# Six weight tiles that began at the same place in a 256-byte line, moved to six different places

## The chip, the core and the metric

The kernel runs on one core of a Trainium2 chip. Its time is the device time of one execution in microseconds (us): lower is better. Each execution does the whole layer, from inputs in device memory to the output in device memory.

The core has a matrix engine (PE, with its weight loads shown apart as PEld), a vector engine (DVE), an activation engine (ACT), a general engine (POOL), a queue that issues transfers (SP), and 16 DMA engines. The four engines work out of one on-chip memory of 128 partitions. "Offset" below always means the byte within a partition at which a tile begins.

## What is computed

One layer of an encoder on 512 frames of 1024 channels, in float32. Cut to its products:

```python
proj = x @ w_in                                    # queries, keys, values, gates of two mixers
y_a = sparse attention (indexer, top 128 keys, relative bias, softmax)   # 8 heads of 64
y_s = stick-breaking attention (strictly causal)                        # 8 heads of 64
merged = sigmoid(g_a + b_a) * (y_a @ w_branch_dsa) + sigmoid(g_b + b_b) * (y_s @ w_branch_sb)
x = layer_norm(alpha * x + merged @ w_out)
u, g = split(x @ w_ffn_in)                         # 2 x 2816 channels
h = gelu(causal_conv3(u)) * g
x = layer_norm(alpha * x + h @ w_ffn_out)
```

## The kernel before, in words

**Products in three passes.** PE takes its operands in a rounded 32-bit format. To keep the accuracy of float32, every operand is split in two: a high part (the value copied into the rounded format) and a low part (the value minus the high part). A product is then three matmuls into one accumulator: high by high, high by low and low by high. So each weight that comes from memory is loaded, split by two elementwise instructions, and used by three matmuls for each slice of 128.

**The stream of weights.** All weights pass through one object, `Stream`, in one fixed order of pieces of up to 128 x 1024 values. `load` (line 75) fetches pieces ahead into the pool `rawp` (three buffers of 128 x 1024 float32), through the SP queue at line 73. `_advance` (line 88) splits them, up to three ahead of their use: line 104 writes the high part on ACT; the low part is written by DVE (line 113), by POOL for the five pieces in `POOL_LO` (the same line), or, for the 14 pieces in `DMA_LO`, by ACT with minus the high part (line 107) and then a DMA that adds the weight itself into the tile (line 110).

**The ring.** The split parts stand in the pool `ring`: three buffers with the tag `whi` and three with the tag `wlo`, allotted at lines 98 and 99. These six buffers are all that the change touches. A few pieces have places of their own instead (`self.place`): the eight of the output projection and eleven of the last 24. Everything else uses the ring.

**Who reads the ring.** As the stationary operand (the weights that PE loads): the projections at lines 312 to 314 (384 columns) and 233 to 235 (512 columns), the branch projections at lines 611 to 613 and 817 to 819, and the feed-forward input `ffn_in` at lines 937 to 939. As the moving operand (what streams through PE): the value projections at lines 270 to 272 and the feed-forward output, `product`, at lines 1017 to 1019.

**Stages in time.** Up to about 322 us, projections, indexer and both attentions are interleaved: the attention of a head keeps DVE, ACT, POOL and the transposing DMAs (`send_planes`, line 478; `join_planes`, line 487) busy, and projections from the list `FILL` keep PE busy meanwhile. Then come the last gates and the branch products (to about 345 us), the output projection `o_ps` (lines 866 to 868), the first norm, the feed-forward pairs `u`/`g` with the first output products (about 391 to 674 us), the remaining output products (to about 732 us) and the last norm.

**The order on each engine** is set when the program is built, by a list scheduler with a model of times, with ties written by hand (`issue_after`).

**Where tiles lie.** Pools are stacked from the left side in the order in which they are opened: constants, `rawp`, `ring`, and behind them the pools of each stage (`bp` for the attentions, `cp`, `tp`, then `ep`, `fp`, `hp`, `rp`). Others are stacked from the right side (`xp`, `dp`, `qp`, `wp`). A helper, `padded`, rounds small tiles up to 128 bytes. In the built program each `raw` tile and each of the six ring tiles begins 192 bytes into a line of 256 bytes, since each is 4096 bytes long.

Of the kernel before, what the change touches and what calls it, by code (L numbers as in the profile page):

```python
# [12 lines left out]
F32R = mybir.dt.float32r  # L13
# [35 lines left out]
def r32(ap):  # L49
    return ap.bitcast(F32)  # L50


class Stream:
# [34 lines left out]
    def _advance(self, upto):  # L88
        nc = self.nc
        n = len(self.pieces)  # L90
        self.load(min(n, upto + self.al))
        while self.ns < min(n, upto + self.asp, self.nl):
            t, w = self.loaded.pop(self.ns)
            key = self.pieces[self.ns][0]
            if key in self.place:
                hi, lo = self.place[key](key)
            else:
                hi = self.ring.tile([128, 1024], F32R, tag="whi", name=f"whi_{self.ns}")
                lo = self.ring.tile([128, 1024], F32R, tag="wlo", name=f"wlo_{self.ns}")
            after = None  # L100
            if key in self.prepare:
                w, after = self.prepare[key](t)
            with self.tc.issue_after(self.behind) if self.behind is not None else nullcontext():
                self.high = nc.scalar.activation(hi[:, :w], t[:, :w], AF.Copy).ins  # L104
            self.behind = None
            if key in self.lo_by_dma:
                self.high = self.highs[key] = nc.scalar.activation(lo[:, :w], r32(hi[:, :w]), AF.Copy, scale=-1.0).ins
                if key == "gb6":
                    self.behind = self.high
                self.done[key] = nc.gpsimd.dma_start(lo[:, :w], self.pieces[self.ns][1], accum_op=ALU.add).ins  # L110
            else:
                eng = nc.gpsimd if key in self.lo_on_pool else nc.vector
                self.done[key] = eng.tensor_sub(lo[:, :w], t[:, :w], r32(hi[:, :w])).ins  # L113
            if after is not None:
                after()
            self.split[self.ns] = (hi, lo)
            self.ns += 1
# [1181 lines left out]
```

## Times and profile before

| | |
|---|---|
| two timed runs | 746.85 and 747.27 us, median 747.06 us |
| span of the profiled execution, first to last instruction | 744.9 us |
| PE busy | 735.6 us, 99% |
| DVE busy | 572.0 us, 77% |
| ACT busy | 408.0 us, 55% |
| POOL busy | 148.8 us, 20% |
| mean granted PE clock | 0.998 |

The profiled execution's own time is its span, 744.9 us; the median of the timed runs is 2.2 us longer, which is what lies before the first and after the last profiled instruction. In the rows of the profile, a line number is that of the kernel, `whi<-raw` means that a tile named `whi` is written from one named `raw` (buffer numbers are left out), `x` a count, and the last field of a row the idle time just before the instruction with what ended it. Matmuls overlap, so the duration of one (389 ns) is longer than the step from one start to the next.

### The profile page before, as it was taken

How to read it: one execution, taken by the hardware profiler on the slowest of the kernel's cores; microseconds unless marked ns; L12 is line 12 of the kernel's file. 1: busy time of each engine (PE TensorE's matmuls, PEld its weight loads, DVE VectorE, ACT ScalarE, POOL GpSimd, SP SyncE). 2: the span in 40 equal slices, each digit the busy share in tenths (PEclk: the TensorE clock that was granted, in tenths of full speed). 3: DMA queues.
4: the chain of work that ended last, by engine and by line, in shares of the span. 5: the costliest groups of instructions: out<-in, count | busy, mean ns of one | idle time of the engine just before them, and what ended most of it. 6: DMA issues, size and time to landing. Idle time of an engine off the chain costs nothing.

```text
span 744.9 us, 9755 instructions
## 1 busy us (share of the span) xinstructions
PE 735.6 (99%) x3477; PEld 616.9 (83%) x3477; DVE 572.0 (77%) x907; ACT 408.0 (55%) x572; POOL 148.8 (20%) x161
## 2 busy tenths in 40 slices
PE   9999999999999999999999999999999999999995
PEld 7888888888888888888889888888888888888885
DVE  5569888999679898668755866686767668668985
ACT  6466867797785587845473533443444344345430
POOL 0002224365743332000101111011101101110011
PEclk9999999999999999999999999999999999999999
DMA  7445887796476455527832544444443444448632
GB/s 266 157 128 188 207 172 173 158 214 163 116 181 154 135 126 136 131 85 247 289 57 86 170 141 142 141 143 143 141 166 114 161 136 149 144 140 268 202 130 84
DMA packets 73631, 117.03 MB, mean 157 GB/s; under 512 B 42536, under 2 KB 42792, under 8 KB 73584
## 3 DMA queue, kind: packets, MB, share of 16 engines
q1 hardware_dynamic: 66304, 93.98, 42.0%
q0 software_dynamic: 5744, 18.38, 9.9%
q10 hardware_dynamic: 1536, 4.06, 2.1%
q8 instruction: 27, 0.44, 0.3%
q14 instruction: 20, 0.16, 0.1%
HBM read 95.93 MB, written 9.98 MB: 142 GB/s over the span
## 4 chain that ended last, share of the span: by engine, by line
PE 89%; DVE 3%; POOL 2%; issue 2%; DMA 2%; ACT 2%; DVEq 0%; POOLq 0%; ACTq 0%
PE u_ps L937 5%; PE u_ps L939 5%; PE g_ps L937 5%; PE u_ps L938 5%; PE g_ps L939 5%; PE g_ps L938 5%; PE m L1019 2%; PE m L1017 2%; PE m L1018 2%; PE av_ps L511 2%; PE ga_ps L234 2%; PE ga_ps L233 2%; PE gb_ps L235 2%; PE gb_ps L234 2%; PE ga_ps L235 2%; PE gb_ps L233 2%
## 5 line engine op out<-in xcount | busy, mean ns | idle before, releaser
L104 ACT ACTIVATE whi<-raw 128x1024 fp32r<-128x1024 f32 (+1 forms) x124 | 123.8, 1001 | 143.1 <-PE g_ps L938 43.7
L113 DVE TENSOR_TENSOR wlo<-raw,whi 128x1024 fp32r<-128x1024 f32 (+1 forms) x105 | 123.9, 1181 | 36.3 <-ACT whi L104 35.6
L939 PE MATMUL u_ps<-x1h,wlo 128*128 128x512 f32 (+1 forms) x192 | 71.4, 372 | 0.0
L937 PE MATMUL u_ps<-x1h,whi 128*128 128x512 f32 (+1 forms) x192 | 71.3, 372 | 0.0
L938 PE MATMUL u_ps<-x1l,whi 128*128 128x512 f32 (+1 forms) x192 | 71.3, 371 | 0.0
L937 PE MATMUL g_ps<-x1h,whi 128*128 128x512 f32 (+1 forms) x184 | 69.9, 380 | 0.0
L938 PE MATMUL g_ps<-x1l,whi 128*128 128x512 f32 (+1 forms) x184 | 69.9, 380 | 0.0
L939 PE MATMUL g_ps<-x1h,wlo 128*128 128x512 f32 (+1 forms) x184 | 69.9, 380 | 0.0
L939 PEld LDWEIGHTS u_ps<-x1h,wlo 128*128 128x128 f32 x192 | 36.2, 188 | 6.3
L938 PEld LDWEIGHTS u_ps<-x1l,whi 128*128 128x128 f32 x192 | 36.2, 188 | 6.3
L937 PEld LDWEIGHTS u_ps<-x1h,whi 128*128 128x128 f32 x192 | 36.2, 188 | 6.2
L939 PEld LDWEIGHTS g_ps<-x1h,wlo 128*128 128x128 f32 x184 | 34.6, 188 | 6.6
L938 PEld LDWEIGHTS g_ps<-x1l,whi 128*128 128x128 f32 x184 | 34.6, 188 | 6.5
L937 PEld LDWEIGHTS g_ps<-x1h,whi 128*128 128x128 f32 x184 | 34.6, 188 | 6.5
L960 DVE TENSOR_TENSOR t<-raw 128x512 f32<-128x512 f32 x11 | 7.6, 693 | 40.1 <-DMA raw<-in_w_fo_dram 39.2
L569 POOL TENSOR_TENSOR bm<-win,score 128x256 f32<-128x256 f32 (+2 forms) x24 | 26.9, 1147 | 32.2 <-DMA pl<-bm 27.3
L985 ACT ACTIVATE c<-c,cwt 128x512 f32<-128x512 f32 x22 | 15.9, 725 | 27.5 <-DVE c L984 27.3
L979 POOL MEMSET u<- 128x2 f32 x22 | 2.1, 98 | 143.7 <-ACT whi L104 99.2
L993 DVE TENSOR_TENSOR hF<-g_ps,c 128x512 f32<-128x512 f32 x22 | 15.1, 687 | 19.7 <-PE g_ps L939 19.7
L835 POOL TENSOR_TENSOR rstd<-rstd,mhalf 128x1 f32<-128x1 f32 x8 | 7.7, 959 | 104.6 <-DVE rstd L834 104.6
L423 DVE MAX8 m<-score 128x8 f32<-128x256 f32 (+2 forms) x48 | 26.6, 556 | 0.9
L557 POOL TENSOR_TENSOR beta<-beta,keep 128x1280 f32<-128x1280 f32 x8 | 21.6, 2704 | 26.7 <-DVE keep L554 26.7
(576 smaller groups left out, 2088.3 us busy)
## 6 DMA issues: line engine op xcount, KB each, us to landing
raw<-in_w_fi_dram SPq DMA_DIRECT2D x44, 512.0 KB, 3.3
raw<-in_w_t_dram SPq DMA_DIRECT2D x32, 512.0 KB, 3.7
raw<-in_w_fo_dram SPq DMA_DIRECT2D x26, 512.0 KB, 4.2
wlo<-in_w_t_dram POOLq DMA_DIRECT2D x14, 512.0 KB, 5.8
raw<-in_w_br_dram SPq DMA_DIRECT2D x8, 512.0 KB, 4.0
raw<-in_w_o_dram SPq DMA_DIRECT2D x8, 512.0 KB, 4.1
raw<-in_w_v_dram SPq DMA_DIRECT2D x7, 512.0 KB, 4.6
raw_b<-in_w_fo_dram SPq DMA_DIRECT2D x6, 512.0 KB, 5.5
```

The costliest lines, as they stand in the source:

```text
L104: self.high = nc.scalar.activation(hi[:, :w], t[:, :w], AF.Copy).ins
L113: self.done[key] = eng.tensor_sub(lo[:, :w], t[:, :w], r32(hi[:, :w])).ins
L233: nc.tensor.matmul(ps[:M], wh[:, c], xh[k], start=(k == 0), stop=False)
L234: nc.tensor.matmul(ps[:M], wh[:, c], xl[k], start=False, stop=False)
L235: nc.tensor.matmul(ps[:M], wl[:, c], xh[k], start=False, stop=(k == KC - 1))
L423: nc.vector.max(m8, sc)
L557: nc.gpsimd.tensor_mul(beta, beta, keep[:, 1:ATT + 1])
L569: nc.gpsimd.tensor_add(bm[:, OFF[j]:OFF[j] + N], win[:, 512 - N:512], score[j])
L937: nc.tensor.matmul(ps[:, c], wh[:, kc], x1h[:, k, c], start=(k == 0), stop=False)
L938: nc.tensor.matmul(ps[:, c], wh[:, kc], x1l[:, k, c], start=False, stop=False)
L939: nc.tensor.matmul(ps[:, c], wl[:, kc], x1h[:, k, c], start=False, stop=(k == KC - 1))
L985: nc.scalar.activation(c, c, AF.Gelu_apprx_tanh, bias=cwt[:, f, 3:4])
```

## The change

```diff
@@ -95,8 +95,8 @@
             if key in self.place:
                 hi, lo = self.place[key](key)
             else:
-                hi = self.ring.tile([128, 1024], F32R, tag="whi", name=f"whi_{self.ns}")
-                lo = self.ring.tile([128, 1024], F32R, tag="wlo", name=f"wlo_{self.ns}")
+                hi = self.ring.tile([128, 1032], F32R, tag="whi", name=f"whi_{self.ns}")
+                lo = self.ring.tile([128, 1032], F32R, tag="wlo", name=f"wlo_{self.ns}")
             after = None
             if key in self.prepare:
                 w, after = self.prepare[key](t)
```

Each ring tile becomes 4128 bytes long. What is written and read of it stays the first 1024 values. In the two built programs the instructions of PE, DVE, ACT, POOL and SP, and their order, are the same row for row; only offsets differ:

| tiles | offset within 256 bytes before | after |
|---|---|---|
| `raw` (pool `rawp`) and all constants | 192 (`raw`) | unchanged |
| `whi`, the three buffers in the order in which they lie | 192, 192, 192 | 192, 224, 0 |
| `wlo`, the three buffers in the order in which they lie | 192, 192, 192 | 32, 64, 96 |
| tiles behind the ring that were at 192 (for example `beta`, `win`, `mh`, `bh`, `wo`) | 192 | 128 |
| tiles behind the ring that were at 64 (for example `xr`, `raw_qi`, `q`, `k`, `keep`/`bm`, `pl`, `back`) | 64 | 0 |
| tiles stacked from the right side (`xh`, `xl`, `x1h`, `x1l`, the norm's tiles) | 64 or 192 | unchanged |

Before the change every tile that PE reads begins at a multiple of 64 bytes. After it, one `whi` buffer (224) and two `wlo` buffers (32 and 96) begin 32 bytes off such a multiple.

## The prediction

> **What bounds the kernel now.** First the page's head.
>
> ```profile
> span 744.9 us, 9755 instructions
> PE 735.6 (99%) x3477; PEld 616.9 (83%) x3477; DVE 572.0 (77%) x907; ACT 408.0 (55%) x572; POOL 148.8 (20%) x161
> ```
>
> PE is busy nearly throughout. A busy PE may still run below its best rate, so the second view is the list of PE's waits (total, count, longest).
>
> ```profile
> PE idle_ps L210 <- DVE idle L207: 1.2, 1, 1.2
> PE bs_ps L613 <- DVE wlo L113: 0.3, 1, 0.3
> PE qi_ps L312 <- ACT whi L104: 0.3, 1, 0.3
> ```
>
> Only two waits lie on the ring, 0.3 us each. So the time can change in two ways only: the step from one matmul to the next changes, or some splitting engine becomes late enough that PE waits where it now doesn't. For the step, starts from the timeline of PE: the 24 matmuls of one feed-forward input, 12 of the output projection, and, from the chain of waits, three of 384 columns.
>
> ```profile
> 501.44 0.39 PE L937 MATMUL g_ps<-x1h,whi 128*128 128x512 f32 x1
> 506.88 0.39 PE L937 MATMUL u_ps<-x1h,whi 128*128 128x512 f32 x1
> ```
>
> ```profile
> 380.15 0.39 PE L867 MATMUL o_ps<-wo0l,mh 128*128 128x512 f32 x1
> 382.87 0.39 PE L867 MATMUL o_ps<-wo4l,mh 128*128 128x512 f32 x1
> ```
>
> ```profile
> 11.22 0.52 PE qi_ps L314 x3
> ```
>
> With the ring as weights: 5.44 / 24 = 0.2267 us. Without any ring tile (`wo` and `mh` have places of their own): 2.72 / 12 = 0.2267 us. With 384 columns: 0.52 / 3 = 0.173 us. The 128 columns between are worth 0.053 us, 0.417 ns each, so 512 columns take 213.5 ns and some 13 ns of each step do not depend on the columns.
>
> The step is thus the same to a tenth of a nanosecond whether or not PE reads the ring. In the first stretch the ring is also written: the instructions on `whi` alone, in that window, are these (busy us and count on PE, PEld, DVE, ACT, POOL).
>
> ```profile
> 501.40:506.90 5.50, 4.99 (x18) 3.02 (x18) 1.23 (x1) 1.06 (x1) 0.00 (x0) 1.00 0.72 245
> ```
>
> One split on ACT and one on DVE went on beside 18 matmuls from the same ring. If the common offset made the six tiles collide with each other, the first stretch would be the longer. That is the main evidence that there is nothing here for a new offset to win.
>
> **The change part by part.** Nothing is removed or added, and the order on every engine is the same, so no wait is new and no transfer is issued at another place. What remains is the price of an instruction at another offset, for each reader and writer of the moved tiles.
>
> *Weights on PE.* How long a weight load really takes shows where a matmul is too short to cover it, in five short matmuls of one attention head:
>
> ```profile
> 97.81 0.28 PE L511 MATMUL av_ps<-pth,vs 128*128 128x256 f32 x1
> 97.92 0.28 PE L511 MATMUL av_ps<-ptl,vs 128*128 128x256 f32 x1
> 98.05 0.23 PE L511 MATMUL av_ps<-pth,vs 128*128 128x128 f32 x1
> 98.11 0.27 PE L511 MATMUL av_ps<-ptl,vs 128*128 128x128 f32 x1
> 98.22 1.25 PE L540 MATMUL z_ps<-ks1a,qs1a 128*128 128x512 f32 x7
> ```
>
> 128 columns should take 53 + 13 = 67 ns, and one step is 60 ns, but the next is 110: the load is behind, and takes about 0.11 us. Under a step of 0.2267 it has 0.117 us to spare; even a load twice as long would be hidden there. My estimate for the weights is 0; if loads from shifted tiles were half as long again (0.165), the 384-column steps (0.173) would still cover them.
>
> *Moving operands on PE.* 512 values are 2048 bytes of a row in either case. The trace has no operand of PE off a multiple of 64 bytes. Of the two sorts it has (192, as in the stretches above, and 64, as `vs`, `qs` and `pth` here), neither is slower: two 256-column steps from 97.81 to 98.05 are 0.12 us each, and 256 x 0.417 + 13 = 120 ns. I take 0; the upper bound is the first rival.
>
> *Splits on ACT, DVE and POOL.* These engines do have rows at odd offsets: the convolution reads `u` 4 and 8 bytes past a tile's start (L983, L984), beside the norm's like instruction (L839); ACT writes `u` at 8 bytes (L980), beside a copy to a tile's start (L1155); POOL multiplies by `keep` from 4 bytes on (L557), beside an addition from tiles' starts (L569).
>
> ```profile
> L839 DVE SCALAR_TENSOR_TENSOR r<-r,mv,ln x14: 741/746/751, 363.7 to 734.8; 128x512 f32<-128x512 f32 x14
> ```
>
> ```profile
> L983 DVE SCALAR_TENSOR_TENSOR c<-u,cwt,c x22: 743/750/1401, 406.8 to 670.1; 128x512 f32<-128x512 f32 x22
> ```
>
> ```profile
> L984 DVE SCALAR_TENSOR_TENSOR c<-u,cwt,c x22: 739/752/753, 408.6 to 671.9; 128x512 f32<-128x512 f32 x22
> ```
>
> ```profile
> L980 ACT ACTIVATE u<-u_ps 128x512 f32<-128x512 f32 x22 | 12.8, 581 | 0.0
> L1155 ACT ACTIVATE m<-P 128x512 f32<-128x512 f32 x2 | 1.1, 583 | 0.0
> ```
>
> ```profile
> L557 POOL TENSOR_TENSOR beta<-beta,keep 128x1280 f32<-128x1280 f32 x8 | 21.6, 2704 | 26.7 <-DVE keep L554 26.7
> L569 POOL TENSOR_TENSOR bm<-win,score 128x512 f32<-128x512 f32 x8 | 11.0, 1380 | 0.0
> ```
>
> Medians (the middle of three numbers) of 750 and 752 against 746 ns on DVE; 581 against 583 on ACT; on POOL 2704 / 1280 = 2.1 ns a value against 1380 / 512 = 2.7. So between a gain of nothing and a loss of 6 ns per 512 values on DVE, and no loss on ACT and POOL. I take 0, since a step of 32 bytes is coarser than these. Where it would be paid is the one stretch in which the chain of waits leaves PE (start, length, what):
>
> ```profile
> 189.56 0.19 PE ka_ps L233
> ...
> 191.01 3.63 POOL wlo L113
> ...
> 195.64 0.17 POOL wlo L113
> ...
> 209.95 0.96 ACT whi L104
> ...
> 210.93 1.68 DVE wlo L113
> ...
> 224.85 2.23 DVE wlo L113
> ...
> 228.51 1.22 DVE wlo L113
> ...
> 231.88 5.88 DMA pl<-bm
> ...
> 245.59 3.55 DMA pl<-bm
> ...
> 254.31 1.55 PE l_ps L580 x8
> ```
>
> The splits in it sum to 3.63 + 0.17 + 0.96 + 1.68 + 2.23 + 1.22 = 9.89 us, and the scores `l_ps` at 254.31 wait for its end, so a split longer by some share costs PE that share of 9.89 us. The four splits on DVE and ACT at 6 ns per 512 values, 12 each, cost under 0.05 us. Elsewhere there is cover: in a steady stretch of the feed-forward DVE is busy 70.77 of 100 us and its splits are 26.85 of that (the second row is `wlo` alone), so they could double and still end in time, at 97.6.
>
> ```profile
> 420.00:520.00 100.00, 100.00 (x443) 82.81 (x442) 70.77 (x93) 40.50 (x51) 13.75 (x20) 1.00 0.44 148
> ```
>
> ```profile
> 420.00:520.00 100.00, 57.19 (x148) 27.44 (x147) 26.85 (x24) 0.00 (x0) 0.00 (x0) 1.00 0.44 148
> ```
>
> *Transfers.* Fourteen low parts are finished by a DMA into the ring; and tiles behind the ring move too, among them both ends of the transposes `pl<-bm`:
>
> ```profile
> wlo<-in_w_t_dram POOLq DMA_DIRECT2D x14, 512.0 KB, 5.8
> pl<-bm SPq DMA_TRANSPOSE x16, 3.5
> ```
>
> A 4096-byte row from byte 192 touches 17 lines of 256 bytes; from 32, 64 or 96 it touches 17 as well. So the fourteen should keep their 5.8 us. The transposes go from 64 to 0; no row shows one from a line's start, so I bound them by nothing and by all that PE could win, below.
>
> The Trainium skill, "DMA: Bandwidth & Descriptors", section "How a descriptor splits into AXI transactions", has a rule for this: a descriptor is cut at 256-byte addresses, and one that starts off such an address pays for the bytes before its start. By it a piece of 256 bytes at 64 takes two transactions and at 0 one, so the transposes would shorten. No row here shows it either way; the result would be the second rival's.
>
> *Sum.* Weights 0, moving operands 0, splits 0, transfers 0: the span stays 744.9 us, and with the 2.2 us around it (median 747.06 less 744.9) the time stays **747.1 us**. Without a change in the step, what could add up is small on both sides: minus 0.5 us (the waits before `bs_ps` and `l_ps`) to plus 1 us (a tenth more on the chain's splits), 746.6 to 748.1.
>
> **The rivals.** *1. A row that begins 32 bytes off a multiple of 64 costs PE a second start: slower.* The counts of matmuls on `whi` and on `wlo`:
>
> ```profile
> 0.00:745.00 745.00, 550.61 (x1826) 337.10 (x1826) 134.90 (x118) 148.46 (x151) 14.06 (x5) 1.00 0.54 157
> ```
>
> ```profile
> 0.00:745.00 745.00, 346.79 (x913) 171.17 (x913) 134.90 (x118) 14.73 (x14) 26.32 (x19) 1.00 0.54 157
> ```
>
> One of three `whi` buffers and two of three `wlo` buffers are so placed: 1826 / 3 + 913 x 2 / 3 = 1217 matmuls. At a second 13 ns each that is 15.8 us, all of it on PE: 762.9 us. From 12.3 ns a matmul on (15 / 1217) the kernel is slower by over 2%. For it: nothing in the trace has tried such an offset on PE. Against it: offsets 64 and 192 give the same step, and the other engines read 4 bytes past a start as fast.
>
> *2. The tiles behind the ring gain: slightly faster.* If the two transposes on the chain (5.88 and 3.55 us) took half, the chain would shorten by 4.7 us, but PE wins only what it waits: 0.3 us before L613, and 0.23 before `l_ps`, whose step from the matmul ahead is 254.31 - 253.85 = 0.46 instead of 0.23.
>
> ```profile
> 253.85 0.39 PE L613 MATMUL bs_ps<-ys3h,wlo 128*128 128x512 f32 x1
> ```
>
> That gives 746.5 us.
>
> *3. The splits lengthen the chain: slower within 2%.* A quarter on each of the splits between 191 and 231 us costs 9.89 / 4 = 2.5 us: 749.6 us. For it: this stretch has no slack. Against it: the rows at odd offsets.
>
> *4. The 13 ns are a collision that the change ends: faster.* If the new offsets took them off each of the 1826 + 913 = 2739 matmuls that read the ring, that would be 35.6 us: 711.5 us. For it: the 13 ns are there on every step. Against it: `o_ps` has the same 13 ns without the ring, and 256 columns from the ring-free `pth` too.
>
> The Trainium skill, "TensorE: Matmul & The Clock Gate", section "Back-to-back issue gap", gives N / 2.4 + 2.5 ns, which is 215.8 for 512 columns. By it 10.9 of the 226.7 would be too much, and rival 4 would come to 717.2 us; this trace has 226.7 with and without the ring, so the page's lower figure does not point at the ring.
>
> **How the numbers follow.** Unchanged 0.78, rival 2 0.07, rival 3 0.07, rival 1 0.07 (0.04 of it at over 2%), rival 4 0.01. The prediction is the likeliest, 747.1 us. The range takes in its bounds, rivals 2 and 3 and a small part of rival 1 (3 ns a matmul, 3.7 us, 750.8): 745.5 to 750.8. Below 746.5 it allows 1 us for runs that differ (the two runs are 0.4 apart). Faster by over 2% 0.01, slower by over 2% 0.04, within 2% (about what a measurement of this kernel can tell from no change) 0.95.
>
> **What would show it.** Right: steps of 0.2267 us in 937 to 939 and in 1017 to 1019, medians of L104 and L113 within 1%, the same two short waits of PE. Rival 1 shows as longer steps on a third of the weights' matmuls and two thirds of `wlo`'s, at best in 1017 to 1019. Rival 2 shows as shorter landings of `pl<-bm`, rival 3 as longer L113 or L104 and a larger PE wait near 227 and 254 us. The prediction is wrong if any row at a moved offset differs from its like before by more than a few per cent, or if the span moves by over 4 us.

## The result and the profile after

The changed kernel takes 757.79 us (median of two runs, 757.65 and 757.93) against 747.06: a ratio of 1.0139, with a 95% interval of 1.0120 to 1.0158. It is slower by 1.4%, 10.7 us, and lies outside the predicted range of 745.5 to 750.8. The profiled execution's span went from 744.9 to 755.9 us at the same mean granted clock, 0.998.

The head of the page after, and the whole list of PE's waits:

```profile
span 755.9 us, 9755 instructions
PE 746.9 (99%) x3477; PEld 617.2 (82%) x3477; DVE 570.6 (75%) x907; ACT 408.8 (54%) x572; POOL 148.8 (20%) x161
```

```profile
PE idle_ps L210 <- DVE idle L207: 1.2, 1, 1.2
```

PE is busy 11.3 us longer with the same 3477 matmuls, and both short waits on the ring are gone, as a slower PE gives the splits more time. So nothing is late. The matmuls themselves take longer, and it shows in their groups with shapes kept apart (busy us, mean ns of one); each of these three means was 389 before.

```profile
L937 PE MATMUL g_ps<-x1h,whi 128*128 128x512 f32 x168 | 66.6, 397 | 0.0
L939 PE MATMUL g_ps<-x1h,wlo 128*128 128x512 f32 x168 | 66.1, 394 | 0.0
L938 PE MATMUL g_ps<-x1l,whi 128*128 128x512 f32 x168 | 65.8, 392 | 0.0
```

The weight loads, as the profile records them, did not become longer: each takes 188 ns on average, and only the idle time between loads grew. These are the loads of the high parts for the inputs `g`, before and then after:

```profile
L937 PEld LDWEIGHTS g_ps<-x1h,whi 128*128 128x128 f32 x184 | 34.6, 188 | 6.5
```

```profile
L937 PEld LDWEIGHTS g_ps<-x1h,whi 128*128 128x128 f32 x184 | 34.6, 188 | 7.1
```

Matmuls overlap, so the step from start to start is the price. In the timeline of PE after, these are the first matmuls of four feed-forward inputs, 24 matmuls apart:

```profile
427.60 0.39 PE L937 MATMUL g_ps<-x1h,whi 128*128 128x512 f32 x1
...
433.19 0.40 PE L937 MATMUL u_ps<-x1h,whi 128*128 128x512 f32 x1
...
438.78 0.40 PE L937 MATMUL g_ps<-x1h,whi 128*128 128x512 f32 x1
...
444.33 0.39 PE L937 MATMUL u_ps<-x1h,whi 128*128 128x512 f32 x1
```

The distances are 5.59, 5.59 and 5.55 us, where before 24 matmuls took 5.44. The output projection, whose operands `mh` and `wo` moved together from 192 to 128, did not change at all; 12 of its matmuls:

```profile
383.70 0.39 PE L867 MATMUL o_ps<-wo0l,mh 128*128 128x512 f32 x1
...
386.42 0.39 PE L867 MATMUL o_ps<-wo4l,mh 128*128 128x512 f32 x1
```

That is 2.72 us as before. The steps of all matmuls, summed by the lines of the kernel in both traces (the last column is the difference divided by the count, 256-column and shorter matmuls included):

```
lines                              before    after    difference    a matmul
937-939    feed-forward input      240.49   245.89   +5.40 us      4.8 ns x 1128
233-235    projections             181.46   184.69   +3.23         4.1 ns x 792
1017-1019  feed-forward output     105.09   106.95   +1.86         3.8 ns x 494
270-272    value projections        44.21    44.76   +0.55
312-314    qi, ki                   16.86    17.04   +0.19
611-613, 817-819  branches          44.79    44.71   -0.08
866-868    output projection        43.52    43.55   +0.03
the rest (attention and others)     59.49    59.11   -0.37
sum                                735.91   746.70   +10.8
```

The loss is here, on the lines that read the ring with 512 columns. The branches read it with 512 columns too, and they paid like the others: their median step went from 227 to 232 ns. Their sum stood still only because pauses in their stretch went at the same time: what single steps over 245 ns have above 227 fell from 1.0 to 0.2 us, PE's former wait at L613 among it. The other moved work stood still; the splits and transfers after:

```profile
L104 ACT ACTIVATE whi<-raw 128x1024 fp32r<-128x1024 f32 (+1 forms) x124 | 123.9, 1003 | 162.9 <-PE g_ps L938 48.8
L113 DVE TENSOR_TENSOR wlo<-raw,whi 128x1024 fp32r<-128x1024 f32 (+1 forms) x105 | 124.1, 1184 | 42.4 <-ACT whi L104 41.0
```

```profile
wlo<-in_w_t_dram POOLq DMA_DIRECT2D x14, 512.0 KB, 5.5
pl<-bm SPq DMA_TRANSPOSE x16, 3.3
```

The splits' means were 1001 and 1181 ns, the landings 5.8 and 3.5 us.

### The profile page after: what moved, and what is told of

Its sections match the earlier page's. It is cut to its first block, busy times and chain, and to the rows that moved or that the text cites. A ratio compares the mean times of both kernels' runs of the same rounds, so it can differ in the third digit from the quotient of the medians.

```text
span 755.9 us, 9755 instructions
## 1 busy us (share of the span) xinstructions
PE 746.9 (99%) x3477; PEld 617.2 (82%) x3477; DVE 570.6 (75%) x907; ACT 408.8 (54%) x572; POOL 148.8 (20%) x161
## 4 chain that ended last, share of the span: by engine, by line
PE 93%; DVE 3%; DMA 1%; ACT 1%; issue 1%; ACTq 0%; DVEq 0%
PE g_ps L937 5%; PE u_ps L939 5%; PE u_ps L937 5%; PE u_ps L938 5%; PE g_ps L939 5%; PE g_ps L938 5%; PE m L1017 2%; PE m L1018 2%; PE m L1019 2%; PE av_ps L511 2%; PE ga_ps L233 2%; PE ga_ps L234 2%; PE ga_ps L235 2%; PE o_ps L866 2%; PE o_ps L867 2%; PE o_ps L868 2%
## 5 line engine op out<-in xcount | busy, mean ns | idle before, releaser
L104 ACT ACTIVATE whi<-raw 128x1024 fp32r<-128x1024 f32 (+1 forms) x124 | 123.9, 1003 | 162.9 <-PE g_ps L938 48.8
L113 DVE TENSOR_TENSOR wlo<-raw,whi 128x1024 fp32r<-128x1024 f32 (+1 forms) x105 | 124.1, 1184 | 42.4 <-ACT whi L104 41.0
```

## The experiments

The steps after show a pattern that no rule on single offsets gives. Read by the addresses of the built program, the pieces of the feed-forward use three pairs of buffers, and each pair has its own step, the same every time: `whi` at 192 with `wlo` at 32 gives 232.4 ns (median of 19 inputs), 224 with 96 gives 233.3 (10), and 0 with 64 gives 231.1 (10). Writers, which come at other moments each time, are an unlikely cause of so steady a pattern; the runs without the layer, below, leave them out. And the third pair stands on multiples of 64, where rival 1 sees no price. Three theories were set against each other. **A**: a step is 226.7 ns only where the weights and the moving operand begin at the same place within 256 bytes, and some 4 ns or more longer otherwise. **B** (rival 1): tiles 32 bytes off a multiple of 64 pay. **C**: PE pays for the jump between the places of a piece's high and low tile.

The variants of the whole layer keep the instructions and their order of the kernel before; unused tiles shift what lies behind them. In three kernels (`e5_sweep`, `e8_fine`, `e9_pairs`) the layer is left out: they copy the input to the output and run only matmuls, in sections of 24, from four tiles.

**All six together, but elsewhere.**

```diff
-    ring = ctx.enter_context(tc.tile_pool(name="ring", bufs=3))
+    ctx.enter_context(tc.tile_pool(name="gapa", bufs=1)).tile([128, 16], F32, name="gapa_t"); ring = ctx.enter_context(tc.tile_pool(name="ring", bufs=3)); ctx.enter_context(tc.tile_pool(name="gapb", bufs=1)).tile([128, 48], F32, name="gapb_t")
```

> All six ring tiles begin at the same place again, but at 0 in a line of 256 bytes, while what PE multiplies them with (xh, xl, x1h, x1l, ah, bh) stays at 192; the tiles behind the ring stay where they were. Theory A (a step is 226.7 ns only where the weights and the moving operand begin at the same place within 256 bytes, and some 4 ns longer otherwise): all 2739 matmuls on the ring pay, 2739 x 3.9 = 10.7 us, 757 to 759 us, o_ps unchanged. Theory B (only tiles 32 bytes off a multiple of 64 pay): 747 us, since 0 is a multiple of 64. Theory C (what costs is that high and low tile differ, so that the place of the weights jumps from load to load): 747 us.

Measured: 758.97 us (758.48 to 759.46, four runs), ratio 1.0162, interval 1.0149 to 1.0175. Six tiles at one common place, a multiple of 256 bytes, are as slow as six different places: B and C both fall. Three inputs of the feed-forward in its timeline:

```profile
434.55 0.39 PE L937 MATMUL u_ps<-x1h,whi 128*128 128x512 f32 x1
...
440.15 0.39 PE L937 MATMUL g_ps<-x1h,whi 128*128 128x512 f32 x1
...
445.75 0.39 PE L937 MATMUL u_ps<-x1h,whi 128*128 128x512 f32 x1
```

Each takes 5.60 us, 233.3 ns a step. The feed-forward input loses 6.23 us, the projections 3.69, the output products 1.58. One wait is new here, and is a further 1.3 us of the loss:

```profile
PE vs_ps L270 <- ACT whi L104: 1.3, 1, 1.3
```

**Ring in place, the tiles behind it moved.**

```diff
-    ring = ctx.enter_context(tc.tile_pool(name="ring", bufs=3))
+    ring = ctx.enter_context(tc.tile_pool(name="ring", bufs=3)); ctx.enter_context(tc.tile_pool(name="gapb", bufs=1)).tile([128, 48], F32, name="gapb_t")
```

> The ring as before (all six at 192), but all that lies behind it on the left side 192 bytes further, as the change has it. Theory A: only the feed-forward output products pay, whose operands then differ (bh and ah at 128, ring at 192): 494 x 3.8 ns = 1.9 us, 748.5 to 749.5 us. Theories B and C: 747 us. If it were not the ring at all but the shifted tiles that cost the time: 757.8 us.

Measured: 747.8 us (746.83 to 755.04, 12 runs), ratio 1.0022, interval 1.0006 to 1.0039. The output products, whose weights `bh` and `ah` went to 128 while the ring stayed at 192, lost 0.75 us, less than expected; the feed-forward input is as before (+0.03). The 429 of them with 512 columns went from 226.9 to 229.3 ns a step, and the 65 with 256 columns gained, from 119.5 to 115.2. The sweep below finds this very difference, weights 64 bytes lower than the moving operand, to be a cheap one (229.0 ns). The profiled execution was the one outlier, 755.04 us: a single wait of 5.7 us for the DMA that finishes a low part, and behind it twelve steps of 395 to 591 ns, 2.5 us more than at 227.

```profile
PE gb_ps L235 <- DMA wlo<-in_w_t_dram: 5.7, 1, 5.7
```

The other eleven runs lie between 746.8 and 749.8. Why that transfer landed late once is not settled.

**Nearly everything on 32.** A gap of 24 values ahead of the ring and one of 40 on the right side put the ring, `x1h`, `x1l`, `bh`, `ah` and their like at 32, which is off a multiple of 64 for all of them, and common.

```diff
-    edge = ctx.enter_context(tc.tile_pool(name="edge", bufs=1, side="right"))
+    edge = ctx.enter_context(tc.tile_pool(name="edge", bufs=1, side="right")); ctx.enter_context(tc.tile_pool(name="gapr", bufs=1, side="right")).tile([128, 40], F32, name="gapr_t")
...
-    ring = ctx.enter_context(tc.tile_pool(name="ring", bufs=3))
+    ctx.enter_context(tc.tile_pool(name="gapa", bufs=1)).tile([128, 24], F32, name="gapa_t"); ring = ctx.enter_context(tc.tile_pool(name="ring", bufs=3))
```

> Ring, tiles behind it and the tiles on the right side all moved alike, so that nearly everything PE reads begins at 32 in a line of 256 bytes (the attention tiles, which were at 64, at 160); nothing is 64-byte aligned any more, but all is at the same place relative to each other. Theory A: 747 us (746.5 to 748). Theory B: all ring matmuls pay instead of 1217, 10.7 x 2739 / 1217 = 24 us, 771 us. Theory C: 747 us.

Measured: 746.78 us (746.11 to 748.71, 11 runs), ratio 1.0000, interval 0.9991 to 1.0009. Its feed-forward input in the timeline:

```profile
434.92 0.39 PE L937 MATMUL g_ps<-x1h,whi 128*128 128x512 f32 x1
...
440.36 0.39 PE L937 MATMUL u_ps<-x1h,whi 128*128 128x512 f32 x1
```

5.44 us again. An offset of 32 costs nothing if both operands have it. This is B's plainest refutation: nearly every 512-column matmul has both operands there.

**Low parts 256 bytes further.**

```diff
-                lo = self.ring.tile([128, 1024], F32R, tag="wlo", name=f"wlo_{self.ns}")
+                self.gap = getattr(self, "gap", None) or self.ring.tile([128, 64], F32, tag="gap", bufs=1, name="gap_t"); lo = self.ring.tile([128, 1024], F32R, tag="wlo", name=f"wlo_{self.ns}")
```

> The three low tiles moved 256 bytes further from the high ones (one gap of 256 bytes between them), the rest behind moved by 256 too: addresses differ, places within 256 bytes do not. Theory A with a period of 256 bytes: 747 us. If the distance of high and low tile in itself cost (a period above 256): up to 758 us.

Measured: 747.07 us (746.40 to 747.56, 11 runs), ratio 1.0001, interval 0.9992 to 1.0010. Another 256 bytes between the high and the low tiles cost nothing, where 128 cost 1.05% (below): what counts in these runs is the place within 256 bytes.

**The price by itself.** Weights `wh`, `wl` and moving operands `mh`, `ml`; the shifts a to h are 0, 32, ... 224 bytes.

```diff
+    for i, s in enumerate(STEP):
+        section(f"weights_{s}", 8 * i, 8 * i, 0)      # high and low weights shifted
...
+        section(f"moving_{s}", 0, 0, 8 * i)
...
+        section(f"both_{s}", 8 * i, 8 * i, 8 * i)
...
+        section(f"low_{s}", 0, 8 * i, 0)              # low weights alone
...
+        section(f"narrow_{s}", 8 * i, 8 * i, 0, 256)  # 256 columns; middle_: 384
...
+        section(f"movlow_{s}", 0, 0, 0, 512, 8 * i)   # low moving operand alone
```

> Not the layer: only matmuls of the feed-forward's kind (24 to a section, high by high, high by low, low by high), with no split, no DMA and no other engine beside them, on operands at chosen places; the output is a copy of the input. Seven sets of eight sections, the shift going from 0 to 224 bytes in steps of 32: both weights shifted, the moving operands shifted, both shifted alike, only the low weights shifted, both weights shifted at 256 and at 384 columns, only the low moving operand shifted. Theory A: 226.7 ns in the eight sections with both shifted alike, and in shift 0 of the others; 228 to 236 elsewhere. Theory B: longer at 32, 96, 160, 224 whatever is shifted. Theory C: longer only where the low weights alone are shifted. If ACT, DVE or DMA had a part in it: 226.7 everywhere.

Measured (one execution of 307.01 us; clock 1.0): first matmuls of sections, in the timeline of PE.

```profile
20.76 0.39 PE L157 MATMUL weights_a<-mh,wh 128*128 128x512 f32 x1
...
26.21 0.39 PE L157 MATMUL weights_b<-mh,wh 128*128 128x512 f32 x1
...
31.80 0.40 PE L157 MATMUL weights_c<-mh,wh 128*128 128x512 f32 x1
...
37.40 0.39 PE L157 MATMUL weights_d<-mh,wh 128*128 128x512 f32 x1
```

```profile
115.36 0.39 PE L157 MATMUL both_b<-mh,wh 128*128 128x512 f32 x1
...
120.83 0.39 PE L157 MATMUL both_c<-mh,wh 128*128 128x512 f32 x1
...
126.31 0.39 PE L157 MATMUL both_d<-mh,wh 128*128 128x512 f32 x1
```

With equal places 24 matmuls take 5.45 us, with the weights alone 32 or 64 bytes further 5.59 and 5.60, with both operands 32 or 64 bytes further 5.47 and 5.48. The means of the steps inside each section, its first step left out, in ns:

```
shift in bytes             0      32     64     96     128    160    192    224
weights, 512 columns     226.7  233.2  233.4  234.1  233.4  233.5  229.0  233.3
moving operand           226.7  233.3  228.9  233.9  233.3  234.0  233.3  233.0
both                     227.6  227.7  227.7  227.7  227.7  227.7  227.7  227.7
low weights alone        227.7  233.4  231.4  232.7  231.2  233.5  231.5  231.3
low moving op. alone     227.7  232.1  231.9  231.1  233.0  232.4  230.0  231.2
weights, 384 columns     173.3  173.3  174.7  173.3  176.3  176.6  173.3  176.6
weights, 256 columns     120.0  118.4  117.8  117.2  118.4  119.9  117.7  117.8
```

The second row is the first read backwards from 0, to 0.4 ns: a moving operand 64 bytes further is the same as weights 192 bytes further. So what counts is the difference. The first column has the same places in all its sections of 512 columns and still 226.7 or about 227.7, so 1 ns is not from the places. No other engine works here, and no transfer of data, so the price is PE's own reading. With 256 columns a difference gains about 2 ns instead. The layer shows that too: its 209 matmuls of 256 columns on lines 937 to 939 and 1017 to 1019 went from 120.5 to 119.0 ns a step with the change.

**Low parts alone 128 bytes off.** The gap of the fourth experiment with 32 values instead of 64, and 32 values behind the ring.

```diff
-                lo = self.ring.tile([128, 1024], F32R, tag="wlo", name=f"wlo_{self.ns}")
+                self.gap = getattr(self, "gap", None) or self.ring.tile([128, 32], F32, tag="gap", bufs=1, name="gap_t"); lo = self.ring.tile([128, 1024], F32R, tag="wlo", name=f"wlo_{self.ns}")
...
-    ring = ctx.enter_context(tc.tile_pool(name="ring", bufs=3))
+    ring = ctx.enter_context(tc.tile_pool(name="ring", bufs=3)); ctx.enter_context(tc.tile_pool(name="gapb", bufs=1)).tile([128, 32], F32, name="gapb_t")
```

> The three low tiles at 64 instead of 192 (128 bytes off the high ones and off all else), the rest in place. Theory A with a period of 256 bytes: the matmuls on low tiles pay, and by the trace of the change their neighbours too: 750 to 758 us. With a period of 128 bytes or less: 747 us. Theory B: 747 us. Theory C: as theory A, 750 to 758.

Measured: 754.94 us (754.31 to 755.72, four runs), ratio 1.0105, interval 1.0091 to 1.0119. The feed-forward's steps are 231.0 ns (median over 39 inputs); the sweep's low weights at 128 gave 231.2. Its groups:

```profile
L939 PE MATMUL g_ps<-x1h,wlo 128*128 128x512 f32 x168 | 66.7, 397 | 0.0
L938 PE MATMUL g_ps<-x1l,whi 128*128 128x512 f32 x168 | 66.5, 396 | 0.0
L937 PE MATMUL g_ps<-x1h,whi 128*128 128x512 f32 x168 | 65.4, 389 | 0.0
```

The pass on `x1l` and `whi` pays too, although both of its own operands are still at 192: its mean step is 232.4 ns, that of line 939 234.1, that of line 937 226.8. The sweep's section, taken pass by pass, has the same: 232.4, 234.3 and 226.6. So the rule has to be taken over neighbours. The steps that pay are that of the matmul that uses the shifted tile and that of the matmul just before it. While a matmul streams, the profile has the load of the next weights: for line 938 that is the shifted `wlo`, but for line 939 it is `whi`, at the common place, and line 939 pays as well. So a meeting of that load with the streaming does not explain both, and no run separates the two.

**All pairs of high and low.**

```diff
+    for i in range(8):
+        for j in range(8):
+            section("pair_" + STEP[i] + STEP[j], 8 * i, 8 * j, 0)   # high weights, low weights
```

> As the sweep, with high and low weights shifted apart: all 64 pairs of 0 to 224 bytes, the moving operands at 0. Theory A: 226.7 only where both are at 0. The change's three pairs (0 and 96, 32 and 128, 64 and 160 from the moving operand) should give what its feed-forward steps show, 232.4, 233.3 and 231.2 ns, with no ACT, DVE or DMA at work. If writers had a part in the change's loss, these pairs come out shorter here.

Measured (one execution): of 64 pairs only 0 with 0 gives 226.7 ns; all others lie between 228.8 and 235.3. Eight further sections shift the low weights and the low moving operand alike and leave the high parts: 227.7 ns at 0 and 230.7 to 232.8 elsewhere, so it does not help to move the low parts alone, even together. The expectation took the buffers' pairs in the order in which they lie; the program pairs 192 with 32, 224 with 96 and 0 with 64, which against a moving operand at 192 are the shifts (0, 96), (32, 160) and (64, 128): sections `pair_ad`, `pair_bf` and `pair_ce`, each followed by its neighbour.

```profile
37.35 0.39 PE L157 MATMUL pair_ad<-mh,wh 128*128 128x512 f32 x1
...
42.93 0.39 PE L157 MATMUL pair_ae<-mh,wh 128*128 128x512 f32 x1
...
93.01 0.40 PE L157 MATMUL pair_bf<-mh,wh 128*128 128x512 f32 x1
...
98.61 0.40 PE L157 MATMUL pair_bg<-mh,wh 128*128 128x512 f32 x1
...
132.15 0.40 PE L157 MATMUL pair_ce<-mh,wh 128*128 128x512 f32 x1
...
137.70 0.40 PE L157 MATMUL pair_cf<-mh,wh 128*128 128x512 f32 x1
```

5.58, 5.60 and 5.55 us; inside the sections the steps are 232.7, 233.4 and 231.0 ns. The layer has 232.4, 233.3 and 231.1. The offsets alone thus give the step of each of the change's three pairs to 0.3 ns, without the layer around them. This pairing was set after the run, but the passes bear it out one by one (high by high, low moving operand, low weights): `pair_ce` has 236.0, 228.3 and 229.0 ns, its inputs in the layer 235.7, 228.3 and 229.3, and `pair_bf` 233.3, 233.7 and 233.0 against 233.7, 233.3 and 233.0.

**A search in steps of 4 bytes.**

```diff
+    for i in range(64):
+        section("fine_" + STEP[i // 8] + STEP[i % 8], i, i, 0)
+    for i in range(64):
+        section("slim_" + STEP[i // 8] + STEP[i % 8], i, i, 0, 256)
```

> As the sweep before (24 matmuls to a section, no layer, the output a copy of the input), now with both weights shifted against the moving operands in steps of 4 bytes from 0 to 252, at 512 columns and again at 256. Theory A: at 512 columns 226.7 ns at shift 0 and, if the loss comes in whole pieces of 32 bytes or more, the same 226.7 up to some first step; 229 to 234 elsewhere. If some place within 256 bytes beat the common one, it shows here as a section under 226 ns. At 256 columns 117 to 120 as before, 120 at shift 0.

Measured (one execution): a shift of 4 bytes already gives 232.3 ns. Nearly all lie between 228 and 236, the worst (164 bytes) at 238.0 and the next (212) at 236.6; a few single shifts (120, 144, 156, 204, 228, 252) are at 226.6 or 226.7 like 0, and none is below. With 512 columns no shift tried wins anything beyond the common place.

**The attention's tiles brought to 192.** Before, the attention's tiles stand at 64 and meet tiles at 192 here and there.

```diff
-    rbf = padded(bp, [32, H], name="rbf")
+    rbf = bp.tile([32, 64], F32, name="rbf")[:, :H]
```

> The kernel before with one small tile (rbf) 128 bytes longer, so that the attention's tiles (k, q, v, the turned weights), which were at 64, begin at 192 like all else that PE reads. Theory A: in the first 322 us the steps of 512 columns that were over 227 ns (3.2 us over in all) fall back to 227: 744 to 746 us, faster than the kernel before. Theories B and C, or no effect of the place: 747 us.

Measured: 746.33 us (745.93 to 747.37, 11 runs), ratio 0.9992, interval 0.9983 to 1.0001: not clear of no change, and the gain that was expected did not come. What steps have over 227 ns in the first 322 us fell only from 3.2 to 2.8 us in all (steps from one 512-column matmul to the next, without a wait). What the rest comes from, these runs do not show.

**The six tiles alone.** The change, and 16 values behind the ring that put everything else back on its old place.

```diff
-                hi = self.ring.tile([128, 1024], F32R, tag="whi", name=f"whi_{self.ns}")
-                lo = self.ring.tile([128, 1024], F32R, tag="wlo", name=f"wlo_{self.ns}")
+                hi = self.ring.tile([128, 1032], F32R, tag="whi", name=f"whi_{self.ns}")
+                lo = self.ring.tile([128, 1032], F32R, tag="wlo", name=f"wlo_{self.ns}")
...
-    ring = ctx.enter_context(tc.tile_pool(name="ring", bufs=3))
+    ring = ctx.enter_context(tc.tile_pool(name="ring", bufs=3)); ctx.enter_context(tc.tile_pool(name="gapb", bufs=1)).tile([128, 16], F32, name="gapb_t")
```

> The change with a gap of 64 bytes behind the ring, so that all tiles behind it begin where they did before within 256 bytes, and only the six ring tiles differ. Theory A: all of the loss but the part on the output products' other operands, 756 to 758.5 us. If the shifted tiles behind the ring made part of it: 747 to 755.

Measured: 757.20 us (756.84 to 757.65, four runs), ratio 1.0134, interval 1.0117 to 1.0151, which takes in the change's 1.0139. In its timeline:

```profile
433.27 0.40 PE L937 MATMUL u_ps<-x1h,whi 128*128 128x512 f32 x1
...
438.87 0.40 PE L937 MATMUL g_ps<-x1h,whi 128*128 128x512 f32 x1
...
444.42 0.39 PE L937 MATMUL u_ps<-x1h,whi 128*128 128x512 f32 x1
```

5.60 and 5.55 us, as with the whole change. One detail differs: the pair 224 with 96 has 231.3 ns in nine of its ten inputs and 233.4 in the first, which is the one shown, where the change had 233.3 or 233.4 in all ten, and the feed-forward input loses 4.90 us instead of 5.40. So one and the same pair of places can settle at two steps. The loss belongs to the six tiles; the tiles behind them add nothing that can be measured.

## Why the prediction was wrong

**The step that failed** is the one on PE's moving operands: "Of the two sorts it has (192 [...] and 64 [...]), neither is slower [...]. I take 0", and with it the "Weights 0" of the sum. It asked what an operand's own offset costs. The price depends on the offset of the weights against that of the moving operand, and every steady row quoted had the two at one place: `whi` and `x1h` at 192, `mh` and `wo` at 192, `vs` and `pth` at 64. Rows without any difference can't price a difference. The same holds for the chief argument, that the step is 0.2267 us with and without the ring: true, and true for the same reason in both. The cost of that term is not 0 but 10.7 us, 3.9 ns over the 2739 matmuls that read the ring.

**Weights** were taken as hidden as long as a load is shorter than a step, since a load twice as long would still be covered. The sweep shows steps of 233 ns with no wait at all, so the cover by length was not what decided: a shifted tile lengthens a step that has room for its load. The cover was also smaller than it says: 0.11 us is the distance of two loads that follow closely, where the profile's record of a single load has 188 ns, of a step of 226.7. By the records, a load twice as long would not have been hidden. It did not come to that, since they have 188 ns after the change too.

**Rival 1** had the right engine and sign at 0.07, but its condition and its price were both wrong: 32 bytes off a multiple of 64 costs nothing (the third experiment), an even pair costs as much as an odd one (the first), and the price in the feed-forward input is 4 to 7 ns on the mean of the 512-column matmuls of every piece, not 13 ns on 1217 of them (the 3.9 ns above are a mean that takes in the 256-column matmuls, which gained). The 3 ns a matmul that the range took from it, on those 1217, ended at 750.8: too little on too few. Rival 1's argument against itself, "offsets 64 and 192 give the same step", was the same oversight.

**What held.** Splits: L104 and L113 within 0.3% of before, so rival 3 is out. Transfers: the transposes moved a little in rival 2's direction, and PE's two short waits are gone, together worth no more than the 0.6 us of those waits. The median landing of `pl<-bm` is 3.3 and 3.4 us in the two runs with its tiles at 0 (the change and the second experiment) and 3.5 us in the kernel before and the other six runs of the layer. That the transposes are shorter from 0 than from 64 agrees in sign with the Trainium skill, "DMA: Bandwidth & Descriptors", section "How a descriptor splits into AXI transactions"; a piece in one transaction rather than two did not come near to half the time here. The fourteen low parts (5.8 to 5.5 us) show nothing: their median lies between 5.5 and 6.8 us in the runs of the layer, and is 6.2 to 6.7 in three that leave the ring at 192. Rival 4 is out for these matmuls: with 512 columns no shift in any sweep went below 226.6 ns. With 256 columns single shifts took up to 6.7 ns off a step (113.3 against 120.0), so the 13 ns are not all fixed there. The figure that the prediction worked out by the Trainium skill, "TensorE: Matmul & The Clock Gate", section "Back-to-back issue gap" (215.8 ns for 512 columns), is there the gap of an isolated matmul; for a stream of weight loads and matmuls that section has about 131 ns. Neither was reached in any of the 64 shifts of the search, where each matmul has a weight load of its own; the lowest mean was 226.6 ns.

**What stays open** is the cause inside PE or the memory. The runs show a price that depends on the difference of two read addresses within 256 bytes, down to 4 bytes, and steps that settle at 226.7 at equal places and at a few others, or at one of two values for the same places. That two streams of reads hinder each other when they are out of step fits this, but is argued and not shown.

## What to carry to other kernels

Judge a tile's place against that of its partner: here, tiles of weights and of moving operands that meet in back-to-back matmuls of 512 columns, low parts included, belong at the same offset within 256 bytes, and padding that breaks this cost 1.4% with no instruction changed. Tiles in a row keep it by themselves when each is as long as a multiple of 256 bytes. And when a row is used to show that something costs nothing, make sure that the row contains the thing: here all of them had equal offsets.

## What the runs showed of the hardware that was not expected

- The step of a 512-column matmul with its own weight load is 226.7 ns where both operands begin at one place within 256 bytes, wherever that is (226.7 to 227.7 at all eight places tried), and 229 to 235 at the other places in steps of 32 bytes.
- A shift of a single value, 4 bytes, already costs 5.6 ns (232.3), but six of the 63 shifts (120, 144, 156, 204, 228 and 252 bytes) cost nothing.
- The sign depends on the width. With 384 columns a difference costs 0 to 3.3 ns, with 256 columns the common place is among the slower ones (120.0), and single shifts (52, 64, 76 and 88 bytes among them) reach 113.3 to 114.1 in the search; the same 64 bytes had 117.8 in the sweep, so the low values are not fixed by the places alone.
- A tile off the common place lengthens the step of the matmul ahead of it too: with the low weights alone 128 bytes off, the pass ahead of theirs has 232.4 ns, where it has 226.7 with all at one place.
